# A two-block transformer step on one core: the weight ring begins 32 bytes lower, at a multiple of 64 bytes

## The chip, the cores and the metric

One core of a Trainium2 chip runs the program. The metric is the time of one execution on the device in microseconds (us). Three runs of the kernel before were timed; their median is 1489.44 us.

## The reference

256 tokens of width 1024 pass, in float32, through two blocks that follow one another. The first has a mixer (windowed attention with sinks and an HGRN recurrence, both gated, then `w_out`) and a layer of product-key experts: 128 x 128 experts, of which each token takes 8 x 16. The second has a mixer of three parts (gMLP, a convolution, an xLSTM cell), cross attention to a memory of 256 tokens, and a gated feed-forward of width 2816. Cut to the lines that make the large products:

```python
aq, ak, av, hq, hf, hi, hg, ga, gh = split_combined(h @ w_in)
merged = sigmoid(ga) * (y_attn @ w_attn_proj) + sigmoid(gh) * (y_hgrn @ w_hgrn_proj)
x = x + merged @ w_out
x = x + peer_layer(rms_norm(x, norm_ffn_g), w_peer_q, peer_keys, peer_u, peer_v)
...
h = h + hybrid_mixer(hn, w_in[l], ..., w_out[l])
h = h + cross_attention(hn, mn, w_xq[l], w_xkv[l], w_xo[l])
h = h + conv_glu(hn, w_up[l], conv_f_w[l], conv_f_b[l], w_down[l])
```

## The kernel before, in words

All weights, and all experts' rows (every expert is computed, the gates are zero where it isn't chosen), stream through the core as 448 tiles of 128 x 1024 float32 values, each of them a **slot** of work. A ring of pools holds them: four places `wraw` for what the sync queue loads, four places `wh` for the high part that ScalarE rounds off (float32r), three places `wl` for the rest that VectorE subtracts (`Slots`, L259). Every product is made of three matmuls in float32r, one for each of high x high, high x low and low x high; the second operand is kept in two tiles too, named with H and L. A slot of form `form2` or `formv` has 8 x 3 = 24 matmuls of 128 x 128 weights, taken from the ring, on 256 moving columns; `form2h` is the same with two halves of 512 rows. In `form1` it is the other way round: the activations are the weights of the array, and the ring tile is moved (the hi, av and mv slots, the last for the memory's values). Four of the memory's key slots (mk4 to mk7) use plain float32 and no split.

The activations that are moved: `hH`, `hL` (tile `hh`, L346), used by nearly all slots of the first block, by the experts and by most of the second; `yaH/L`, `yhH/L`, `mH/L` for pa, ph and wo of the first block; `yH/L`, `oH/L`, `h5H/L`, `fah/fal` for wo, xo, up (ug, uv) and down (dn) of the second; `hmH/L` for the memory. In the feed-forward the first up slots still move `hH/L`, and from the sixth on `h5H/L`.

The order in which the instructions are issued is worked out beforehand by a planner with estimated times of the engines (`Clock`, L117; pieces of work beside the slots are generators, `go` and `step`). It doesn't look at addresses. L219 is the helper through which nearly every instruction is recorded, so lines say little in the profile, and tiles are told apart by their names. Before the first slot 40 records of products of `ident` with itself run on TensorE (`WARM`, L353 to L356).

Where the tiles lie in a partition, in bytes, as the program allocates them (each tile is rounded up to 32 bytes; `con` comes first, the ring `wp` behind it, then the pools of the stages; a second stack of pools, with `hm` and the keys and values of the memory in it, is filled from the upper end and does not depend on what lies below):

| tile | first byte | modulo 64 | modulo 256 |
|---|---|---|---|
| x | 16512 | 0 | 128 |
| sm (265 columns, 1060 bytes) | 24704 | 0 | 128 |
| hH, hL | 25792, 33984 | 0 | 192 |
| ones_d (1 column) | 42176 | 0 | 192 |
| ident | 42208 | 32 | 224 |
| wraw, wh, wl (4096 bytes each) | 44000, 60384, 76768 | 32 | 224 |
| h5H, oH, second yH; h5L, oL, mL; fah, fal; yL | 89056; 97248; 118752, 121824; 121056 | 32 | 224 |
| yaH, yaL | 122432, 126528 | 0 | 64 |
| yhH, yhL; mH | 167616, 171712; 184000 | 0 | 192 |
| hmH, hmL (upper stack) | 192992, 201184 | 32 | 224 |

The 128 columns of a weight operand are 512 bytes of a partition, the 256 moving columns 1024 bytes, and the slices of a tile begin at multiples of these, so a slice lies as its tile does.

Of the kernel before, what the change touches and what calls it, by code (L numbers as in the profile page):

```python
# [22 lines left out]
F32 = mybir.dt.float32  # L23
# [6 lines left out]
PSUM = bass.MemoryType.PSUM  # L30

T = 256
# [27 lines left out]
# the weight tiles in the order of their use  # L60
# [22 lines left out]
# products of the memory are float32 ones, which take TensorE longer but spare the other engines the splits  # L83
# [24 lines left out]
# log1p(z) / z on [0, 1], relative error 3e-8  # L108
# [4 lines left out]
# y: bits of v -> a first guess of v ** -0.5; y * (w * (w + b) + a) with w = v * y * y comes within 2e-5 of it  # L113
# [3 lines left out]
class Clock:  # L117
    """Estimated times of the engines (ns), by which the order of issue is chosen."""

    # from the end of an instruction to the begin of one that depends on it: the own engine, PE, others  # L120
# [16 lines left out]
    def new(self, ap):  # L137
        """a tile takes the place of an older one of its tag"""
        t = ap.tensor
        if ap.name not in self.floor:  # L140
            ring = self.ring.setdefault(t.tag, [])
            f = 0.0
            if len(ring) >= (t.tag_meta.bufs or 1):
                old = ring.pop(0)
                f = max([r[4] for r in self.writes.pop(old, [])] + [r[4] for r in self.reads.pop(old, [])] + [0.0])
            ring.append(ap.name)
            self.floor[ap.name] = f
            self.writes[ap.name], self.reads[ap.name] = [], []
# [9 lines left out]
    def start(self, e, out, ins):  # L158
        """when an engine could begin"""
        t = self.t[e]  # L160
        for ap in ins + [out]:
            self.new(ap)
        for ap in ins:
            s = self.span(ap)
            for r in self.writes.get(ap.name, ()):
                if self.over(r, s) and not (e == "PE" and r[5] == "PE"):
                    t = max(t, r[4] + self.lat(r[5], e))
        s = self.span(out)
        t = max(t, self.floor[out.name])
        for recs in (self.writes, self.reads):  # L170
            for r in recs.get(out.name, ()):
                if r[5] != e and self.over(r, s):
                    t = max(t, r[4] + self.lat(r[5], e))
        return t
# [34 lines left out]
class Engine:  # L209
    """Hands instructions on to an engine and keeps its estimated clock."""  # L210
# [48 lines left out]
class Slots:  # L259
    """The stream of weight tiles: loads and splits run ahead of the products."""  # L260
# [43 lines left out]
    def done(self, n):  # L304
        """slot n has been issued"""
        if self.raw.pop(n, None) is not None:
            self.dma(len(self.seq))


def build(tc, xT, memT, smalls, smalls2, w1, keysT, uT, vT, w2, outT, stop=None):  # L310
# [22 lines left out]
    x = con.tile([128, 8, T], F32, name="x")  # L333
    sm = con.tile([128, NSM], F32, name="sm")
# [12 lines left out]
    ones_d = con.tile([128, 1], F32, name="ones_d")  # L347
# [5 lines left out]
    # products of nothing while the first loads are under way: they raise the clock of TensorE  # L353
# [8 lines left out]
    def go(g, late=1, eng="VS"):  # L362
        """start a piece of work that is issued bit by bit between the products; what it yields names the
        engines that the next bit is for"""
# [11 lines left out]
    def step(force=False):  # L376
        """issue what is ready by now, as far as the engines keep up"""
# [20 lines left out]
    def tt(out, a, b, op):  # L398
        """elementwise on SBUF: on the engine that is done first"""
# [7 lines left out]
    def until(*keys, eng=None):  # L407
        """for a generator: wait for what others issue"""
# [9 lines left out]
    class Sem:  # L418
        """PSUM tiles of one tag that generators may hold across slots"""
# [20 lines left out]
    def take_v(k=2):  # L440
        """banks for a product over several slots"""
# [20 lines left out]
    def slot(name, mm, evac):  # L462
        """one weight tile: mm(w) -> psum, evac(psum)"""
# [19 lines left out]
    def form2p(a):  # L483
        """float32 products, without splits"""
# [9 lines left out]
    def form2h(a):  # L494
        """two column tiles of a 512-row weight"""
# [9 lines left out]
    def form1(a, pv, i, e, width):  # L505
        """e contraction chunks of `width` columns; pv[t] accumulates over the tiles, both in one bank when they fit"""
# [19 lines left out]
    def pair(names, a, evacs, then=None, block=1, order=range(8), key=None):  # L526
        """two slots whose products alternate per chunk, for operands that are just being made"""
# [14 lines left out]
        # of the last chunks the low parts come last  # L542
# [32 lines left out]
    def formv(acc, a, first, last):  # L575
        """acc[n, t] += w[:, n]^T a, one chunk of the contraction"""
# [26 lines left out]
    def stat_mm(pc, sqs, first=True, last=True):  # L603
        """token sums: pc[t, i] += sum over partitions, for the two halves of the tokens"""
# [8 lines left out]
    def rsqrt_cols(dst, src, e, scale=1.0, E=None):  # L613
        """(src * scale + e) ** -0.5 on a few columns"""
# [4 lines left out]
    def rsqrt_of(dst, vv, E):  # L619
        """vv ** -0.5: a first guess from the bits, a step of third order and one of Newton's"""  # L620
# [25 lines left out]
    def rows_of(dst, cols, n=2):  # L646
        """dst[:, k * 128 + t] = cols[t, k] on all partitions"""
# [5 lines left out]
    # The products run on x * g; 1 / rms scales what comes out of them, until the operand has been  # L653
    # replaced by the normalized one (or for all products of a norm).
# [5 lines left out]
    class Norm:  # L660
        """The scale of a norm: products that come before it is known are scaled when it is."""
# [12 lines left out]
        def chain(self, sqs, e=EPS):  # L674
            """a generator: from the squares to the scale"""
# [24 lines left out]
        def when(self, f, late=1):  # L700
            """start f(rst) as soon as there is one"""
# [5 lines left out]
        def to(self, dst, *fs, late=1):  # L707
            """evacuation, and what to start then"""
# [21 lines left out]
        def renorm(self, src, g, np_):  # L730
            """a generator: the normalized operand, to be put in place of the other one"""
# [11 lines left out]
        def renorm_to(self, src, g, pool, dst, flag):  # L743
            """a generator: the normalized operand in a place of its own"""
# [10 lines left out]
        def write(self, must=False):  # L755
            """between two slots, when the operand is there"""
# [9 lines left out]
    class Sums:  # L766
        """sum over chunks of the squares, for chunks that come one by one"""
# [24 lines left out]
    def residual(n, sums, g, scale=None, key=None):  # L792
        """evacuation that adds to the stream; the operand and the squares of the next norm follow"""
# [23 lines left out]
    # ================= first block: mixer =================  # L817
# [14 lines left out]
    # attention bias: -slope * distance inside the window, -1e30 outside  # L832
# [9 lines left out]
    # scan reset: zero where a chunk of 32 begins  # L842
# [3 lines left out]
    # [s, t]: t >= s in the same chunk of 32  # L846
# [136 lines left out]
    def g_hgrn():  # L983
# [9 lines left out]
        # twice silu; the norm takes care of the factor  # L993
# [20 lines left out]
    def g_hpair(g):  # L1014
# [77 lines left out]
        # half of 1 / rms(po / 2), for the doubled gate  # L1092
# [76 lines left out]
    # the gates are (1 + tanh(z / 2)) / 2; the half follows where the products of wo come out  # L1169
# [51 lines left out]
    # ================= first block: product-key experts =================  # L1221
# [34 lines left out]
    def top16(vals, idx, src, n):  # L1256
        """the 16 largest of each row of the two sources, sorted, and their places"""
# [61 lines left out]
    # the two lists are sorted, so the best 16 sums lie where (a + 1)(b + 1) <= 16: rows 0..3 whole,  # L1319
    # and four columns of rows 4..15  # L1320
# [44 lines left out]
    def g_decode(t):  # L1365
        """key numbers of the chosen pairs"""
# [7 lines left out]
        # rows 0..3: a = pos >> 4, b = pos & 15; after them a = pos >> 2 less 12, b = pos & 3  # L1374
# [61 lines left out]
    def onehots(g):  # L1436
# [4 lines left out]
        for q in range(NG):  # L1441
            i2, gg = idxT[1][:, t + q:t + q + 1], idxT[2][:, t + q:t + q + 1]
            if q % 2 and clock.t["S"] < clock.t["V"] + 500:
                # g * max(1 - |j - i2|, 0)
# [82 lines left out]
    # for the sums of x ** 2 and (x * g4) ** 2  # L1527
# [23 lines left out]
    # keep t >= s  # L1551
# [10 lines left out]
    # the weights of the gates, split  # L1562
# [41 lines left out]
    # ================= second block: mixer =================  # L1604
# [12 lines left out]
    def finish(c0, c1):  # L1617
        """the sums of the experts: stream, operand and squares"""
# [16 lines left out]
    def g_norm3():  # L1635
        """the last norm of the first block and the first of the second"""
        # of x * r1 * g4 with r1 = (m1 + e) ** -0.5 the norm's scale is (r1 ** 2 * m2 + e) ** -0.5, together
        # (m2 + e * (m1 + e)) ** -0.5
# [45 lines left out]
    def gates():  # L1684
        """input and forget gates, tokens on partitions"""
# [12 lines left out]
    def g_gt(p):  # L1698
# [11 lines left out]
        # log sigmoid: min(x, 0) - log1p(exp(-|x|)); log1p(z) / z by a polynomial on [0, 1], to 3e-8  # L1710
# [40 lines left out]
    # causal depthwise convolution along time, taps w[:, 0..n-1]  # L1751
# [17 lines left out]
    def g_xc(h):  # L1769
# [11 lines left out]
        # twice silu  # L1781
# [20 lines left out]
    # conformer: convolution shared between VectorE and GpSimd, group standardize, silu  # L1802
    yb = [mp.tile([128, T], F32, name=f"bg{i}") for i in range(2)]

    def ev_tanh(dst, key, scale=0.5):
        """tanh(z / 2) + 1, which is twice the sigmoid"""
# [14 lines left out]
    # the gates are doubled, the taps halved  # L1821
# [65 lines left out]
    # gMLP  # L1887
# [42 lines left out]
    # xLSTM cell, one head  # L1930
# [155 lines left out]
    # ================= second block: cross attention =================  # L2086
# [72 lines left out]
    # ================= second block: gated feed-forward =================  # L2159
# [96 lines left out]
def _cols(v, n):  # L2256
    """[n*128] -> [128, n]"""
# [3 lines left out]
def _form2(w):  # L2261
    """[K, N] -> [N/128 tiles][128][K/128 * 128]"""
# [4 lines left out]
def _form1(w):  # L2267
    """[1024, N] -> [tiles][128][c, N] with 1024/N chunks per tile"""
# [5 lines left out]
def pack(inp):  # L2274
# [26 lines left out]
    # head i beside head i + 4  # L2301
# [18 lines left out]
    def taps(a, n):  # L2320
        """[K, n*128] -> [128, n*K]"""
# [66 lines left out]
```

## Time and profile before

| | |
|---|---|
| runs | 1487.21, 1489.44, 1493.71 us (median 1489.44) |
| span of the profiled execution | 1484.4 us; its time with what lies around the span is not given |
| TensorE: matmuls in flight, weight loads in flight | 1447.5 us, 1420.5 us |
| VectorE, ScalarE, GpSimd busy | 1076.2, 849.9, 181.4 us |
| transfers | 242.64 MB, 163 GB/s over the span |

The span is from the first to the last instruction. TensorE's matmuls and weight loads are pipelined: a record is longer than the distance to the next one, so rows of the timeline are read here by their first column, the time at which an instruction starts. Records name out<-moving,weights.

### The profile page before, as it was taken

How to read it: one execution, taken by the hardware profiler on the slowest of the kernel's cores; microseconds unless marked ns; L12 is line 12 of the kernel's file. 1: busy time of each engine (PE TensorE's matmuls, PEld its weight loads, DVE VectorE, ACT ScalarE, POOL GpSimd, SP SyncE). 2: the span in 40 equal slices, each digit the busy share in tenths (PEclk: the TensorE clock that was granted, in tenths of full speed). 3: DMA queues.
4: the chain of work that ended last, by engine and by line, in shares of the span. 5: the costliest groups of instructions: out<-in, count | busy, mean ns of one | idle time of the engine just before them, and what ended most of it. 6: DMA issues, size and time to landing. Idle time of an engine off the chain costs nothing. (4 is left out here: it accounts for less than half of the span.)

```text
span 1484.4 us, 30208 instructions
## 1 busy us (share of the span) xinstructions
PE 1447.5 (98%) x11904; PEld 1420.5 (96%) x11904; DVE 1076.2 (73%) x2096; ACT 849.9 (57%) x1617; POOL 181.4 (12%) x228
## 2 busy tenths in 40 slices
PE   8999999999999999999999999999999999999997
PEld 8789999999999999999999999999998899999996
DVE  7866579799888999955555566555699774785665
ACT  4754454454699988844444455444575544654553
POOL 6100032014200000000000030000035420410000
PEclk9999999999999999999999999999999999999998
DMA  6334554555544444455666665666542553556552
GB/s 217 128 114 157 171 185 153 175 172 182 161 141 143 143 143 143 142 180 172 185 188 185 227 198 185 186 185 186 168 129 81 162 159 114 170 185 187 183 184 73
DMA packets 66381, 242.64 MB, mean 163 GB/s; under 512 B 7360, under 2 KB 7488, under 8 KB 65856
## 3 DMA queue, kind: packets, MB, share of 16 engines
q1 hardware_dynamic: 65664, 237.01, 50.4%
q0 software_dynamic: 432, 3.58, 0.7%
q8 instruction: 93, 1.52, 0.4%
q14 instruction: 48, 0.39, 0.1%
q10 hardware_dynamic: 144, 0.14, 0.1%
HBM read 239.64 MB, written 1.05 MB: 162 GB/s over the span
## 5 line engine op out<-in xcount | busy, mean ns | idle before, releaser
L219 ACT CAST wh<-wraw 128x1024 fp32r<-128x1024 f32 x444 | 463.5, 1045 | 239.0 <-PE v L219 119.1
L219 DVE TENSOR_TENSOR wl<-wraw,wh 128x1024 fp32r<-128x1024 f32 x444 | 555.3, 1254 | 57.4 <-issue 41.0
L219 PE MATMUL v<-hH,wh 128*128 128x256 f32 x2048 | 587.0, 287 | 0.8 <-ACT hH L219 0.8
L219 PE MATMUL v<-hH,wl 128*128 128x256 f32 x2048 | 577.7, 282 | 1.4 <-DVE wl L219 1.3
L219 PE MATMUL v<-hL,wh 128*128 128x256 f32 x2048 | 576.6, 282 | 1.9 <-POOL hL L219 1.8
L219 PEld LDWEIGHTS v<-hL,wh 128*128 128x128 f32 x2048 | 386.2, 189 | 3.1 <-POOL hL L219 2.8
L219 PEld LDWEIGHTS v<-hH,wl 128*128 128x128 f32 x2048 | 386.3, 189 | 2.9 <-DVE wl L219 2.6
L219 PEld LDWEIGHTS v<-hH,wh 128*128 128x128 f32 x2048 | 386.9, 189 | 1.0 <-ACT hH L219 1.0
L219 PE MATMUL mm<-hH,wh 128*128 128x256 f32 x656 | 189.6, 290 | 6.7 <-DVE au L219 3.8
L219 PE MATMUL mm<-hH,wl 128*128 128x256 f32 x656 | 184.6, 282 | 2.2 <-DVE wl L219 2.2
L219 PE MATMUL mm<-hL,wh 128*128 128x256 f32 x656 | 183.0, 283 | 3.0 <-DVE hL L219 2.5
L219 PEld LDWEIGHTS mm<-hH,wh 128*128 128x128 f32 x656 | 124.5, 190 | 11.6 <-issue 4.6
L219 PEld LDWEIGHTS mm<-hL,wh 128*128 128x128 f32 x656 | 123.5, 190 | 4.2 <-DVE hL L219 3.1
L219 PEld LDWEIGHTS mm<-hH,wl 128*128 128x128 f32 x656 | 124.3, 189 | 2.8 <-DVE wl L219 2.8
L219 DVE TENSOR_TENSOR hL<-bigA,hH 128x256 fp32r<-128x256 f32 x72 | 31.2, 434 | 85.1 <-ACT hH L219 85.1
L219 PE MATMUL mm<-h5H,wh 128*128 128x256 f32 x272 | 77.0, 283 | 0.0
L219 PE MATMUL mm<-h5L,wh 128*128 128x256 f32 x272 | 77.0, 283 | 0.0
L219 PE MATMUL mm<-h5H,wl 128*128 128x256 f32 x272 | 77.0, 283 | 0.0
L219 DVE TENSOR_TENSOR hL<-bigB,hH 128x256 fp32r<-128x256 f32 x56 | 23.7, 425 | 69.0 <-ACT hH L219 69.0
L219 ACT ACTIVATE ohB<-ohB,gT,ngT 128x128 f32<-128x128 f32 x126 | 62.3, 494 | 4.2
L219 ACT ACTIVATE bigA<-v 128x256 f32<-128x256 f32 (+14 forms) x72 | 25.7, 357 | 68.1 <-PE v L219 68.1
L219 DVE TENSOR_TENSOR ohA<-iota,i1T 128x256 f32<-128x256 f32 x128 | 53.8, 420 | 14.0 <-PE aux L219 6.8
(545 smaller groups left out, 2414.2 us busy)
## 6 DMA issues: line engine op xcount, KB each, us to landing
wraw<-w_dram SPq DMA_DIRECT2D x192, 512.0 KB, 3.6
wraw<-uT_dram SPq DMA_DIRECT2D x128, 512.0 KB, 3.6
wraw<-vT_dram SPq DMA_DIRECT2D x128, 512.0 KB, 3.6
s2t<-smalls_dram POOLq DMA_DIRECT2D x1, 1444.0 KB, 10.9
x<-xT_dram SPq DMA_DIRECT2D x4, 256.0 KB, 6.0
kyT<-keysT_dram POOLq DMA_DIRECT2D x1, 1024.0 KB, 7.1
xm<-memT_dram POOLq DMA_DIRECT2D x1, 1024.0 KB, 5.8
outT_dram<-z SPq DMA_DIRECT2D x4, 256.0 KB, 2.6
```

Source lines behind the costliest of these rows:

```text
L219: r = f(out, *a, **k)
```

## The change

The column `ones_d`, which holds 1/1024 and is multiplied with squares to sum them over the partitions, had a tile of its own between `hL` and `ident`. It becomes column 265 of the tile `sm`, whose 266 columns (1064 bytes) are rounded up to the same 1088 bytes as before. So `ident` and all that lies behind it, the ring `wp` and the pools of the stages with it, begin 32 bytes lower: the ring at 43968, 60352 and 76736 (modulo 64: 0; modulo 256: 192), the tile behind it at 89024. `x`, `sm`, `hH`, `hL` and the upper stack stay. The load of `sm` writes the first 265 columns only. All comments and docstrings are removed too, with empty lines in their place. The diff without these:

```diff
-    sm = con.tile([128, NSM], F32, name="sm")
+    smo = con.tile([128, NSM + 1], F32, name="sm")
+    sm = smo[:, 0:NSM]
     nc.scalar.dma_start(sm, smalls)
...
     hh = (con.tile([128, 8, T], F32R, name="hH"), con.tile([128, 8, T], F32R, name="hL"))
-    ones_d = con.tile([128, 1], F32, name="ones_d")
+    ones_d = smo[:, NSM:NSM + 1]
     V.memset(ones_d, 1.0 / D)
```

## Rows read from the trace of the kernel before

**Rows 1.** The page, part 1: busy time, share of span, instructions.
```profile
PE 1447.5 (98%) x11904; PEld 1420.5 (96%) x11904; DVE 1076.2 (73%) x2096; ACT 849.9 (57%) x1617; POOL 181.4 (12%) x228
```
**Rows 2.** Windows: stretch, its length, busy us and instructions by engine, clock, DMA, GB/s.
```profile
222.00:395.00 173.00, 167.87 (x1387) 165.31 (x1386) 160.44 (x494) 82.17 (x132) 45.23 (x23) 0.99 0.54 170
395.00:690.00 295.00, 294.99 (x2515) 294.78 (x2513) 250.18 (x514) 239.68 (x570) 0.00 (x0) 1.00 0.48 150
```
**Rows 3.** Groups of TensorE: shapes, count, busy us, mean ns, idle before.
```profile
L219 PE MATMUL v<-hH,wh 128*128 128x256 f32 x2048 | 587.0, 287 | 0.8 <-ACT hH L219 0.8
...
L219 PE MATMUL mm<-hH,wh 128*128 128x256 f32 x656 | 189.6, 290 | 6.7 <-DVE au L219 3.8 <-DVE x L219 0.8 <-DVE q L219 0.7
...
L219 PE MATMUL mm<-h5H,wh 128*128 128x256 f32 x272 | 77.0, 283 | 0.0
```
**Rows 4.** Timeline of TensorE (start us, length us): feed-forward slots with hH, first and last.
```profile
1309.29 0.28 PE L219 MATMUL mm<-hH,wh 128*128 128x256 f32 x1
...
1314.85 0.28 PE L219 MATMUL mm<-hH,wl 128*128 128x256 f32 x1
```
**Rows 5.** Timeline of TensorE: the next two up slots, with h5H, first and last.
```profile
1317.83 0.28 PE L219 MATMUL mm<-h5H,wh 128*128 128x256 f32 x1
...
1323.47 0.28 PE L219 MATMUL mm<-h5H,wl 128*128 128x256 f32 x1
```
**Rows 6.** Timeline of TensorE: value slots of the memory, third, ninth and last.
```profile
1167.82 0.28 PE L219 MATMUL mm<-wl,hmH 128*128 128x256 f32 x1
...
1168.53 0.28 PE L219 MATMUL mm<-wl,hmH 128*128 128x256 f32 x1
...
1171.77 0.28 PE L219 MATMUL mm<-wl,hmH 128*128 128x256 f32 x1
```
**Rows 7.** Timeline of TensorE: av slots, third matmul and last.
```profile
1099.20 0.28 PE L219 MATMUL mm<-wl,hH 128*128 128x256 f32 x1
...
1101.65 0.28 PE L219 MATMUL mm<-wl,hH 128*128 128x256 f32 x1
```
**Rows 8.** Timeline of weight loads: 28 of st (32 moving columns), and the next.
```profile
99.19 3.21 PEld L219 LDWEIGHTS aux<-hq,st 128*128 128x128 f32 x28
102.32 0.19 PEld L219 LDWEIGHTS mm<-hH,wh 128*128 128x128 f32 x1
```
**Rows 9.** Timeline of weight loads: hH, hL under 16 or 8 columns, second and last.
```profile
1072.70 0.19 PEld L219 LDWEIGHTS aux<-gw,hL 128*128 128x128 f32 x1
...
1076.04 0.19 PEld L219 LDWEIGHTS aux<-gw,hL 128*128 128x128 f32 x1
```
**Rows 10.** The page, part 5: the subtraction that makes wl.
```profile
L219 DVE TENSOR_TENSOR wl<-wraw,wh 128x1024 fp32r<-128x1024 f32 x444 | 555.3, 1254 | 57.4 <-issue 41.0
```
**Rows 11.** Timeline of all engines at the start.
```profile
0.86 0.06 DVE L219 MEMSET ones_d<- 128x1 f32 x1 [0.86 <-PEq L2379]
...
1.45 7.00 PE L356 MATMUL aux<-ident 128*128 128x128 f32 x40 [1.45 <-DVE ident L219]
...
5.21 1.04 POOL L219 TENSOR_TENSOR sq<-x 128x512 f32<-128x512 f32 x1 [4.07 <-DMA x<-xT_dram]
...
9.40 2.52 POOL L219 TENSOR_TENSOR sq<-x 128x512 f32<-128x512 f32 x2 [0.97 <-DMA x<-xT_dram]
```
**Rows 12.** Transfers: out<-in, queue, count, KB each, median us from issue to landing.
```profile
wraw<-w_dram SPq DMA_DIRECT2D x192, 512.0 KB, 3.6
...
sm<-smalls_dram ACTq DMA_DIRECT2D x1, 132.5 KB, 4.5
```
**Rows 13.** Timeline of TensorE: pa slots, first matmul and last (96).
```profile
132.13 0.28 PE L219 MATMUL mm<-yaH,wh 128*128 128x256 f32 x1
...
143.52 0.28 PE L219 MATMUL mm<-yaH,wl 128*128 128x256 f32 x1
```
**Rows 14.** Timeline of TensorE: first ph slot, first matmul and last (24).
```profile
157.84 0.28 PE L219 MATMUL mm<-yhH,wh 128*128 128x256 f32 x1
...
160.56 0.28 PE L219 MATMUL mm<-yhH,wl 128*128 128x256 f32 x1
```

## The prediction

> **What bounds the kernel now.** I read the page's busy shares first: TensorE has a matmul in flight for 98% of the span and a weight load for 96%, VectorE is at 73% [rows 1]. A busy TensorE need not be a TensorE at its best, so the second view is the windows by stage. [...] So the end is set by how closely matmuls follow one another, and the third view is the timeline of TensorE alone, read for the distance between the starts of neighbours (the "spacing"). Nearly all matmuls are of one shape, 128x128 weights and 256 moving columns. Of these 3 x 2048 + 3 x 656 = 8112 move hH or hL against ring weights; 3 x 272 move h5H or h5L [rows 3]. By the code, at 24 matmuls a slot, the 22 down slots move fah and fal (528), and 8 slots each move yH/yL and oH/oL (384 together). A nanosecond of spacing on the 8112 is 8.1 us.
>
> **The change part by part.** No engine instruction is added or taken away. What changes is where operands lie. In what follows "even" means beginning at a multiple of 64 bytes, "odd" at 32 past one. Before, every ring tile is odd, hH and hL are even and don't move; h5, fa, y and o are odd and become even; the even operands of the first block (ya, yh, mH) become odd. The trace of before holds three of the four combinations of moving operand and weights in the same shape:
> - moving even, weights odd: 47 steps take 1314.85 - 1309.29 = 5.56 us, 118.3 ns each [rows 4];
> - moving odd, weights odd: in the very next pair of slots, same code with h5 in place of hH, 47 steps take 5.64 us, 120.0 ns each [rows 5]; the memory's value slots, where the ring moves and hmH/hmL are the weights, settle, after 6 steps of 118.3 (0.71 us), at 27 steps in 3.24 us, again 120.0 [rows 6];
> - moving odd, weights even: the av slots, same code as the value slots but with hH/hL as weights, 21 steps in 2.45 us, 116.7 [rows 7].
>
> So even weights were worth 120.0 - 116.7 = 3.3 ns, an even moving operand 120.0 - 118.3 = 1.7 ns. Even with even does not occur in this shape; it is what the change makes of the 8112. The lower bound is the spacing where next to nothing moves and only weight loads set the pace: 28 loads of st, odd, in 102.32 - 99.19 = 3.13 us, 111.8 ns [rows 8], and 30 steps of even hH/hL weights in 3.34 us, 111.3 [rows 9]. These two also say that alone a weight load does not care where it begins; the loss arises where both operands are read at once. The upper bound is 120.0 [rows 5]: it could even get worse. I take the sum of the two effects, 118.3 - 3.3 = 115.0 ns, as both neighbours of the missing corner (116.7 and 118.3) lie below the odd-odd corner and nothing in the rows shows the two gains to exclude one another. It follows:
> - the 8112: 8112 x 3.3 ns = 26.8 us less;
> - h5, fa, y, o go from odd-odd to even-even: (816 + 528 + 384) x 5.0 ns = 8.6 us less;
> - pa, ph and the first wo (16 slots, 384 matmuls) gain 3.3 by the weights and lose 1.7 by the moving operand: 0.6 us less;
> - the memory's slots and the hi and av slots (hm doesn't move, the ring does): 4 split key slots of 24 x 3.3 ns; 8 value and 2 av slots of 24 and 4 hi slots of 12 x 1.7 ns: 0.8 us less.
>
> Together 36.8 us, all on the path, since TensorE is the path. What is late next: VectorE. From 395 us on it has 15% and more to spare. From 222 to 395 us it has 7%; there 1387 matmuls x 3.3 ns = 4.6 us are to be won, and I give back half, 2.3 us, as sorting steps come one behind the other. Left: 34.5 us.
>
> The splits write and read the ring too: 444 subtractions of 1254 ns on VectorE [rows 10]. No row shows one with even tiles, so I take no change; if they moved by as much as the matmuls, 4%, either way, it would be 1387 / 24 = 58 slots x 1.254 us x 4% = 2.9 us in the tight stage, and nothing elsewhere. The loads land 3.6 us after issue [rows 12], with four tiles in the ring at 24 x 118.3 ns = 2.84 us a slot, so a slot of 24 x 115.0 = 2.76 us still finds its tile.
>
> The constant column: its memset runs at 0.86 us today, ahead of ident, and ident ahead of the 40 warming products of 7.00 us in TensorE's order [rows 11]. If the wait were set by whole tiles, the memset would have to wait for the load of sm, which lands 4.5 us after its issue [rows 12], so at 4.5 us at the earliest, and ident, the warming products and the first real product behind them would slip by 4.5 - 0.9 = 3.6 us or a little more. But the parts of x, loaded by four transfers into one tile, release their readers one by one, at 5.21 and at 9.40 us [rows 11]; parts of a tile are followed separately, and the column is no part of what is loaded. I take 0, with some 4 us as the upper end, at 1 in 10.
>
> Sum against the profiled execution: its span is 1484.4 us; what lies around it isn't given for that execution, but the median of the three runs, 1489.44, is 5.0 us above. 1484.4 - 34.5 = 1449.9, and 5.0 on top 1454.9: **1455 us**, 2.3% less. By the two bounds of the missing corner: at 111.6 ns 8112 x 6.7 + 1728 x 8.4 ns and some 5 us for the rest are 74 us, less about 7 that VectorE keeps, so 1422 us; at 120.0 ns 8112 x 1.7 = 13.8 us more, 1503 us.
>
> **The rivals.**
> *No change, 1489 us.* The differences of 1.7 and 3.3 ns could come from the order of the products or from which buffers are filled meanwhile. For it: the value slots run 6 steps at 118.3 before they settle at 120.0 [rows 6], so the spacing has a history and not only an address; and ya, which is even, runs at (143.52 - 132.13) / 95 = 119.9 ns [rows 13], not 118.3 as hH and as yh, in the same form of slot, with 23 steps in 2.72 us [rows 14]. Against it: 120.0 is exact over 48 matmuls in a row and hH has 118.3 in the neighbouring slots.
> [...]
> *Slower, 1503 us.* What counts is not where each operand begins but how far they are apart, modulo 256 bytes: the two readers then meet in the same part of the memory in step. By the addresses, h5, fa, y and o lie 0 from the ring, modulo 256, and so do hmH/hmL: all at 120.0. hH and yh lie 32 before it (118.3), the av slots 32 behind (116.7), and ya 96 behind, at 119.9, which the even-or-odd reading doesn't explain [rows 13]. The change moves the ring by 32 and leaves hH: they then lie 0 apart, and 8112 matmuls go to 120.0, while h5, fa, y, o keep their distance and their 120.0: 8112 x 1.7 ns = 13.8 us more. It decides as soon as the even-even corner is over 118.3. [...]
> *Only one effect pays, 1470 to 1481 us.* Even weights alone (116.7 for 118.3 on the 8112, 3.3 on the 1728): 13.0 + 5.7 us less, 1471; less still if VectorE takes back more.
> *No loss left, 1422 us*: the bound of rows 8 and 9.
>
> **How the numbers follow.** 1455 and about it (1443 to 1470) has a chance of 0.50; one effect alone 0.10; no loss left 0.05; no change 0.18; slower 0.17. So faster by over 0.5% 0.65, within 0.5% 0.18, slower by over 0.5% 0.17; 0.5%, some 7 us, is about what a measurement of this kernel can tell from no change. The range from 1425 to 1492 leaves out the slower case and a part of the lowest.
>
> **What would show it.** In the timeline, the hH slots of the feed-forward at 115.0 ns and the h5 slots at the same value; the expert stage without holes and shorter by 2.8%; VectorE's share in the sorting stage up; hH and h5 alike at 120.0 would show the slower rival, 118.3 and 120.0 unchanged the first one; warming products that start past 5 us would show the wait on sm. The forecast is wrong if the even-even spacing lies outside 113 to 117 ns, or if holes appear before wl in TensorE's timeline that eat what the spacing gives.

## The result, and the profile after

The changed kernel takes 1500.76 us (median of 6 runs, 1496.32 to 1504.55), the kernel before 1490.17 us (median of 6). The ratio is 1.0066, with a 95% interval of 1.0045 to 1.0087: some 10 us slower, where 1455 us had been forecast. The profiled execution's span is 1494.8 us, 10.4 us more than before, and every engine gets its instructions in the same order: only addresses differ.

Page, part 1, of the kernel after (engine, busy us, share of the span, instructions); it answers to [rows 1]:
```profile
PE 1459.5 (98%) x11904; PEld 1433.6 (96%) x11904; DVE 1076.2 (72%) x2096; ACT 849.1 (57%) x1617; POOL 181.5 (12%) x228
```
The extra time is TensorE's own, 1459.5 - 1447.5 = 12.0 us; VectorE and ScalarE do what they did. Two stretches of the kernel after in the windows view, beside [rows 2]:
```profile
222.00:395.00 173.00, 167.61 (x1369) 165.49 (x1369) 160.16 (x493) 81.03 (x129) 45.77 (x23) 0.99 0.53 165
395.00:690.00 295.00, 295.00 (x2504) 295.00 (x2503) 250.32 (x516) 240.26 (x574) 0.00 (x0) 1.00 0.49 150
```
In the same 173 us TensorE has 1369 matmuls in flight at some time where it was 1387; VectorE's share, which was to rise, doesn't (160.16 for 160.44). In the expert stage, still without a hole, 2504 for 2515. The granted clock is what it was (0.99 and 1.00).

TensorE's timeline after (start us, length us): the two up slots with hH, the two with h5, the value slots, the av slots, pa and ph, each by its first and its last matmul; they answer to [rows 4 to 7] and [rows 13, 14]:
```profile
1319.59 0.28 PE L219 MATMUL mm<-hH,wh 128*128 128x256 f32 x1
...
1325.23 0.28 PE L219 MATMUL mm<-hH,wl 128*128 128x256 f32 x1
...
1328.23 0.28 PE L219 MATMUL mm<-h5H,wh 128*128 128x256 f32 x1
...
1333.87 0.28 PE L219 MATMUL mm<-h5H,wl 128*128 128x256 f32 x1
...
1178.20 0.28 PE L219 MATMUL mm<-wl,hmH 128*128 128x256 f32 x1
...
1182.10 0.29 PE L219 MATMUL mm<-wl,hmH 128*128 128x256 f32 x1
...
1109.66 0.28 PE L219 MATMUL mm<-wl,hH 128*128 128x256 f32 x1
...
1112.18 0.28 PE L219 MATMUL mm<-wl,hH 128*128 128x256 f32 x1
...
134.07 0.28 PE L219 MATMUL mm<-yaH,wh 128*128 128x256 f32 x1
...
145.47 0.29 PE L219 MATMUL mm<-yaH,wl 128*128 128x256 f32 x1
...
159.99 0.28 PE L219 MATMUL mm<-yhH,wh 128*128 128x256 f32 x1
...
162.71 0.28 PE L219 MATMUL mm<-yhH,wl 128*128 128x256 f32 x1
```
These rows decide most of the case. The reader divides each difference by its steps and sets beside it the distance of the two operands, moving minus weights, modulo 256 bytes:

| slots | steps | distance before, after | spacing before, after (ns) |
|---|---|---|---|
| hH (rows 4) | 47 | 224, 0 | 118.3, 120.0 |
| h5 (rows 5) | 47 | 0, 0 | 120.0, 120.0 |
| value slots (rows 6) | 33 | 0, 224 | 120 (settled), 118.2 |
| av (rows 7) | 21 | 32, 0 | 116.7, 120.0 |
| pa, with ya (rows 13) | 95 | 96, 96 | 119.9, 120.0 |
| ph, with yh (rows 14) | 23 | 224, 224 | 118.3, 118.3 |

Where both operands moved together (h5, ya, yh) nothing changed, though "odd" and "even" changed places. Where one moved, the spacing is that of the new distance: hH has taken over h5's 120.0, the value slots hH's old 118.2.

By stage, cut at the same work in both kernels (the first product of the sorting, the first and last ohB product, the first gw product), the windows of the kernel before:
```profile
214.37:393.24 178.87, 173.00 (x1429) 170.27 (x1427) 166.95 (x517) 83.74 (x132) 45.69 (x23) 0.99 0.53 168
393.24:627.74 234.50, 234.50 (x2006) 234.50 (x2005) 215.66 (x469) 211.66 (x527) 0.00 (x0) 1.00 0.46 143
627.74:1072.69 444.95, 443.09 (x3739) 442.16 (x3738) 256.05 (x358) 218.25 (x343) 14.42 (x31) 1.00 0.60 187
```
and of the kernel after:
```profile
216.71:396.77 180.06, 174.67 (x1429) 172.41 (x1427) 166.94 (x517) 83.28 (x132) 45.77 (x23) 0.99 0.54 167
396.77:632.10 235.33, 235.33 (x2005) 235.33 (x2004) 215.80 (x469) 211.66 (x527) 0.00 (x0) 1.00 0.47 142
632.10:1082.96 450.86, 448.79 (x3740) 448.00 (x3738) 255.62 (x358) 218.10 (x343) 14.52 (x31) 1.00 0.60 185
```
The sorting takes 1.2 us more, the first half of the expert stage 0.8, its second half 5.9; of the remaining 2.5 us, 1.9 lie ahead of pa, where this execution's granted clock was 0.97 on average and that of before 1.00. Over the whole kernel I averaged the steps of up to 130 ns that follow a matmul of hH or hL: 118.49 ns before (7820 steps), 119.78 after (7797). 8112 x 1.29 = 10.5 us, as much as the spans differ. The steps can also be paired, since the order is the same: the 11260 that last up to 130 ns in both traces are 10.2 us longer together, 10.0 of it behind hH and hL, and all others sum to 0.2 us. So the spacing is the whole of the difference between the two profiled executions.

### The profile page after: what moved, and what is told of

Its sections match the earlier page's. It is cut to its first block, busy times and chain, and to the rows that moved or that the text cites. A ratio compares the mean times of both kernels' runs of the same rounds, so it can differ in the third digit from the quotient of the medians.

```text
span 1494.8 us, 30208 instructions
## 1 busy us (share of the span) xinstructions
PE 1459.5 (98%) x11904; PEld 1433.6 (96%) x11904; DVE 1076.2 (72%) x2096; ACT 849.1 (57%) x1617; POOL 181.5 (12%) x228
## 5 line engine op out<-in xcount | busy, mean ns | idle before, releaser
L219 PEld LDWEIGHTS v<-hL,wh 128*128 128x128 f32 x2048 | 392.7, 192 | 3.2 <-POOL hL L219 2.9
L219 PEld LDWEIGHTS v<-hH,wl 128*128 128x128 f32 x2048 | 392.1, 191 | 2.0 <-DVE wl L219 1.9
L219 PEld LDWEIGHTS v<-hH,wh 128*128 128x128 f32 x2048 | 392.3, 192 | 1.0 <-ACT hH L219 1.0
L219 PEld LDWEIGHTS mm<-hH,wh 128*128 128x128 f32 x656 | 127.8, 195 | 11.0 <-issue 4.5
L219 PEld LDWEIGHTS mm<-hL,wh 128*128 128x128 f32 x656 | 126.9, 195 | 4.2 <-DVE hL L219 3.0
L219 PEld LDWEIGHTS mm<-hH,wl 128*128 128x128 f32 x656 | 127.7, 195 | 1.5 <-DVE wl L219 1.5
```

The costliest lines, as they stand in the source:

```text
L219: r = f(out, *a, **k)
```

## The experiments

Two theories were set against each other. *Distance*: the spacing depends on how far the two operands lie apart, modulo 256 bytes. *Own start* (the prediction's reading): it depends on whether each begins at an even or odd multiple of 32. Others are named where they were tried.

**The spacing by itself, first table.**
```
for name, form, wo, mo in MAP:          # 39 pairs of starts, all twice
    for k in range(96):
        c, q = k // 3 % 8, k % 3
        PE.matmul(p, w[:, a:a + 128], h[:, b:b + 256], ...)
    PE.matmul(g, ident, ident, ...)     # between two groups
```


> This kernel leaves the whole computation out and measures the disputed cost by itself: groups of 96 matmuls (128x128 weights, 256 moving columns, the order of chunks and of high and low parts as in a slot), no other engine at work, each group with its own start of the weights and of the moving operand, in bytes past a multiple of 256; two passes over the list. Distance (modulo 256, moving minus weights): all groups of one distance have one spacing, whatever their absolute start: 120.0 ns at 0, 118.3 at -32 (224), 116.7 at +32, about 119.9 at -96 (160), the other distances open, and the even or odd start counts for nothing. Absolute start (the prediction's reading): weights at 0 with the moving operand at multiples of 64 all 115.0; weights at 32 with it at odd multiples of 32 all 120.0. Traffic of other engines (what is read as address is in truth the loads and the splits): all groups alike, near 112 to 116 ns. With only one chunk in use (groups called one), distances of 256, 512 and 768 behave as 0 if the modulus is 256, otherwise they differ.

Timeline of TensorE in this kernel; a row is a group of 96. Its length holds the last matmul's own 0.28 us and a first step of 0.20 us, so the spacing is (length - 0.48) / 94. In order: both at 0; weights 0 and moving 32; both at 32; weights 32 and moving 224; then one chunk only, 0, 256 and 288 apart:
```profile
17.61 11.76 PE L82 MATMUL w_m__141<-H,W 128*128 128x256 f32 x96
...
29.34 11.45 PE L82 MATMUL w_m__240<-H,W 128*128 128x256 f32 x96
...
110.36 11.76 PE L82 MATMUL w_m__933<-H,W 128*128 128x256 f32 x96
...
180.02 11.15 PE L82 MATMUL w_m__1527<-H,W 128*128 128x256 f32 x96
...
377.06 11.76 PE L82 MATMUL one_w_m__3210<-H,W 128*128 128x256 f32 x96
...
388.80 11.76 PE L82 MATMUL one_w_m__3309<-H,W 128*128 128x256 f32 x96
...
435.43 11.55 PE L82 MATMUL one_w_m__3705<-H,W 128*128 128x256 f32 x96
```
Even with even (first row) and odd with odd (third) have 120.0 alike; even weights give anything from 116.7 to 120.0. The mean of the last 48 steps by distance 0, 32, ... 224: 120.0, 116.7, 117.8, 120.0, 118.6, 118.6, 117.8, 118.3, the same with the weights at 0 and at 32 within 0.1 ns, but for one: distance 192 with the weights at 32 has 113.3 (fourth row, 113.5 with its beginning). One chunk at distances of 256, 512 and 768 has 120.0 as at 0, and at 544 and 800 it has 116.7 as at 32, so the modulus is 256. One group doesn't fit as it stands: 288 (last row) has 117.8 in both passes and not 116.7; 117.8 comes back below as a second value of 32. The kernel gives no other engine any work in these groups, so the spread from 113.3 ns at 192 to 123.3 at 4 arises among TensorE's own matmuls and weight loads. The forecast of 119.9 for distance 160 was my slip of sign: ya lies at 96, where the table has 120.0, as rows 13 have.

**The column alone.**
```
+    pad = con.tile([128, 8], F32, name="pad")
     ones_d = smo[:, NSM:NSM + 1]
```


> The changed kernel with 32 bytes left free ahead of ident: the constant column lies in the tile of the loaded parameters as in the change, but the ring and the pools behind it stay where they were before. Distance or absolute start: as before, 1490 us, ratio 0.998 to 1.002. If the column itself costs (its memset waits for the load of the parameters, 4 us in my estimate): 1494, and a slip of the warming products in the trace.

1490.55 us, ratio 0.9992 (0.9975 to 1.001): the column costs nothing that can be measured. In the trace of the change its memset still runs at 0.86 us and the warming products begin at 1.45:
```profile
0.86 0.06 DVE L219 MEMSET sm<- 128x1 f32 x1 [0.86 <-PEq L2380]
...
1.45 6.93 PE L357 MATMUL aux<-ident 128*128 128x128 f32 x40 [1.45 <-DVE ident L219]
```

**hH moved, the ring left alone.**
```
-    smo = con.tile([128, NSM + 1], F32, name="sm")
+    smo = con.tile([128, NSM + 9], F32, name="sm")
```


> The changed kernel with 32 bytes more in the tile ahead of hH: hH and hL begin 32 bytes higher, the ring and everything behind it lie where they were before the change. So the ring hasn't moved, and hH and the ring lie 0 apart, both at odd multiples of 32. Distance: as slow as the change, ratio 1.005 to 1.008, hH slots of the feed-forward at 119.4 to 120.0 ns, yh at 118.3. If the slowdown comes from the ring's or the lower pools' own place (loads, splits, copies): as before, ratio 0.998 to 1.002, hH slots at 118.3. The even-or-odd reading of the prediction: odd with odd, 120.0, so slower too.

1500.42 us, ratio 1.0052 (1.0034 to 1.007). TensorE's timeline, the up slots with hH:
```profile
1324.14 0.28 PE L219 MATMUL mm<-hH,wh 128*128 128x256 f32 x1
...
1329.78 0.28 PE L219 MATMUL mm<-hH,wl 128*128 128x256 f32 x1
```
5.64 us in 47 steps, 120.0 again. So the slowdown of the change comes back without moving the ring, the loads or the lower pools: what makes it is the distance of hH from the ring. (Own start, odd with odd, would have said the same; the next two part them.)

**All starts by all starts, second table.** As the first, with 8 x 8 starts, 72 matmuls a group, in two passes.

> This kernel too leaves the whole computation out: the table of all 8 starts of the weights by all 8 starts of the moving operand (multiples of 32 past 256), 72 matmuls in the order of a slot for each, twice: pass x with 2 passes of a float32 product of 128 columns between the groups, pass y with 6 of 96 columns, so that the groups begin out of another beat. If distance alone decides: one value to each diagonal of the table, as in the first map: 120.0 at 0, 116.7 at +32, 117.8 at +64 and +192, 120.0 at +96, 118.6 at +128 and +160, 118.3 at +224, in both passes. If the beat out of which a group begins counts as well (the one 113.3 of the first map, against 117.8 at the same distance): some cells of a diagonal differ, and differ between the passes, most of all at +192; the 120.0 of distance 0 holds in all 16 cells. The prediction's even-or-odd reading: no such pattern can come out, since even-even and odd-odd lie on the same diagonals.

Timeline of TensorE; a name gives pass, start of the weights, start of the moving operand (A to H for 0 to 224). Here the spacing is (length - 0.48) / 70:
```profile
17.36 8.88 PE L71 MATMUL x_wAmA<-H,W 128*128 128x256 f32 x72
26.22 8.65 PE L71 MATMUL x_wAmB<-H,W 128*128 128x256 f32 x72
...
43.55 8.87 PE L71 MATMUL x_wAmD<-H,W 128*128 128x256 f32 x72
...
69.93 8.72 PE L71 MATMUL x_wAmG<-H,W 128*128 128x256 f32 x72
...
96.11 8.88 PE L71 MATMUL x_wBmB<-H,W 128*128 128x256 f32 x72
104.96 8.65 PE L71 MATMUL x_wBmC<-H,W 128*128 128x256 f32 x72
...
631.45 8.43 PE L71 MATMUL y_wAmG<-H,W 128*128 128x256 f32 x72
```
Settled (mean of the last 24 steps), distance 0 has 120.0 in 16 of 16 groups, 32 has 116.7, 64 has 117.8, 96 has 120.0 and 224 has 118.3, each in all 16. Two distances have two values: 160 has 118.6 to 118.8 or 117.2 to 117.4 (8 groups each), 192 has 117.8 or 113.3 (7 and 9). The very pair A, G has the one in pass x and the other in pass y, so the addresses alone don't pick between them. The passes differ in what runs between the groups; that this sets a beat which picks the value is a reading, and no run tried it by itself. Own start falls here: even with even and odd with odd share the distances 0, 64, 128 and 192, and those run from 113.3 to 120.0.

**Parity as before, distance 32.**
```
+    for _ in range(2):
+        con.tile([128, 2], F32, name="sd", bufs=2)
     hh = (con.tile([128, 8, T], F32R, name="hH"), ...
+    pad = con.tile([128, 8], F32, name="pad")
```


> The ring and all behind it lie as before the change; two 8-byte columns (sd) move from behind hL to ahead of hH, and the constant column lies with the parameters: hH and hL begin 64 bytes higher, even as before, the ring odd as before, but hH now lies 32 ahead of the ring, modulo 256, and not 32 behind. Distance: hH slots at 116.7 instead of 118.3 ns, 8112 x 1.67 = 13.5 us less, some 1477 us, ratio 0.990 to 0.993; with part of it kept by VectorE in the sorting stage 0.995. Even or odd: nothing changes, ratio 0.998 to 1.002, hH slots at 118.3.

1484.08 us, ratio 0.9956 (0.9937 to 0.9975): own start said no change. The feed-forward's slots settle at 117.9, not 116.7 (5.54 us in 47 steps), and the mean over all hH steps is 117.24: the distance of 32 too has a second value, 117.8, which the third table shows in one pass and the first at 288. So faster by distance, but half as much as forecast.

**Parity as after, distance 64.** The same without the pad.

> The changed kernel with the same two columns moved ahead of hH: the ring even and hH even, as in the change, but 64 apart instead of 0. Distance: 117.8 ns, 8112 x 0.55 = 4.5 us less than before, ratio 0.996 to 0.999, against 1.0066 of the change. Even or odd (an even-even pair is as slow as the change showed it): 1.005 to 1.008.

1486.82 us, ratio 0.9946 (0.992 to 0.9973). Even with even, as in the change, and faster than before, as distance 64 says. The ratio is a little below the forecast 0.996 to 0.999, which its interval reaches; the mean step is 117.54, where 117.8 had been taken. TensorE's timeline, up slots with hH:
```profile
1315.83 0.28 PE L219 MATMUL mm<-hH,wh 128*128 128x256 f32 x1
...
1321.37 0.28 PE L219 MATMUL mm<-hH,wl 128*128 128x256 f32 x1
```
5.54 / 47 = 117.9. With this own start is out: the same parity gave 120.0 in the change.

**Distance 192 for hH.**
```
+    for n in ("rsv", "rst_", "rsu"):
+        for _ in range(2):
+            con.tile([128, 4], F32, name=n, bufs=2)
     hh = (con.tile([128, 8, T], F32R, name="hH"), ...
```


> The changed kernel with six 16-byte columns (rsv, rst_, rsu) moved from behind hL to ahead of hH: hH and hL begin 192 bytes higher, even, the ring even as in the change, 192 apart. Distance, by the second table, where this distance has two settled values: 113.3 ns if the slots fall into the short one (8112 x 5.0 = 40 us less than before, less what VectorE keeps: ratio 0.973 to 0.980), 117.8 if into the long one (4.5 us less, 0.997); a mixture lies between. Even or odd: 1.005 to 1.008, as the change.

1470.31 us, ratio 0.9846 (0.9815 to 0.9876), a mixture of the two values: mean 115.15 ns over the hH steps, h5 still at 120.0.

**Distance 192 for both.**
```
+    con2 = es.enter_context(tc.tile_pool(name="con2", bufs=1))   # opened behind wp
...
-    t = con.tile([128, 4], F32, name="rst_", bufs=2)[:, 0:n]
+    t = con2.tile([128, 4], F32, name="rst_", bufs=2)[:, 0:n]    # rsv, rsu too
```


> The changed kernel with the same six columns in a pool of their own between the ring and the pools behind it: hH stays, the ring begins 192 bytes lower, the lower pools lie as in the change. So hH lies 192 from the ring, modulo 256, and h5, fa, y, o lie 192 from it too, not 0. Distance: as h192 for the 8112, and another 1728 x 2.2 ns = 3.8 us (117.8) to 1728 x 6.7 = 11.5 us (113.3) less: ratio 0.965 to 0.995, h5 slots of the feed-forward at 117.8 or 113.3 instead of 120.0. Even or odd: 1.005 to 1.008, h5 at 120.0.

1457.02 us, ratio 0.9753 (0.9714 to 0.9792). hH's mean is 114.07; h5 has left 120.0 for the long value, 117.8.

**Distance 32 for both.** sd goes into spare columns of the parameters' tile, with one pad of 32 bytes ahead of the ring and one behind it.

> sd lies with the parameters, 32 bytes are left free ahead of ident and 32 behind the ring: the ring is odd, hH even, h5, fa, y, o even, and both lie 32 ahead of the ring, modulo 256. Distance: hH as in h32 (measured there 0.9956), and h5, fa, y, o at 116.7 instead of 120.0 ns, 1728 x 3.3 = 5.8 us less: ratio 0.990 to 0.993, h5 slots at 116.7. Even or odd: h5 gains 1.7 ns only, 2.9 us, hH nothing: 0.998.

1475.4 us, ratio 0.9888 (0.9863 to 0.9914). Timeline of TensorE, two slots with h5:
```profile
1318.82 0.28 PE L219 MATMUL mm<-h5H,wh 128*128 128x256 f32 x1
...
1324.31 0.28 PE L219 MATMUL mm<-h5H,wl 128*128 128x256 f32 x1
```
5.49 / 47 = 116.8 where all kernels with distance 0 have 120.0. The ratio lies just under the forecast 0.990 to 0.993: hH too is at 116.78 here, where the kernel from which the forecast took it has 117.24.

**Distances in steps of 8 bytes, third table.**

> The third table, with the whole computation left out again: distances in steps of 8 bytes from 0 to 248, 72 matmuls each, in three passes that differ in the start of the weights (0, 96 and 192 past 256) and in what runs between the groups. If the distance counts in parts of 32 bytes, the four groups from one multiple of 32 on are alike; if it counts continuously, they differ, with 120.0 at 0 in every pass, and there may be a distance below 116.7 that doesn't have two settled values, as 192 does (113.3 and 117.8). From the first map: 123.3 at 4, 118.7 at 16, 118.3 at 48, 120.0 at 80, 119.2 at 208, 117.1 at 240.

Timeline of TensorE, pass x at distances 72, 112 and 192, pass y at 136, and 112 and 192 in pass z:
```profile
96.22 9.01 PE L71 MATMUL x_Cb<-H,W 128*128 128x256 f32 x72
...
140.66 8.46 PE L71 MATMUL x_Dc<-H,W 128*128 128x256 f32 x72
...
228.72 8.43 PE L71 MATMUL x_Ga<-H,W 128*128 128x256 f32 x72
...
456.03 8.89 PE L71 MATMUL y_Eb<-H,W 128*128 128x256 f32 x72
...
730.21 8.45 PE L71 MATMUL z_Dc<-H,W 128*128 128x256 f32 x72
...
826.96 8.72 PE L71 MATMUL z_Ga<-H,W 128*128 128x256 f32 x72
```
The distance counts in steps finer than 32: settled values run from 113.3 (112; its rows of 8.46 us give 114.0 with the beginning) to 122.2 (136, in passes x and z; 120.0 in pass y). Only 112 has 113.3 in all three passes; 192 has it in two (pass z: 8.72, so 117.7), and 16 and 144 have it in pass z alone, where x and y have 118.7 to 118.8. So two values are no peculiarity of 160 and 192: the passes also part at 8, 32, 56 and 128. The value of 0 is 120.0 in all three.

**Distance 112 for both.**
```
-    hh = (con.tile([128, 8, T], F32R, name="hH"), con.tile([128, 8, T], F32R, name="hL"))
+    hb = con.tile([128, 16 * T + 8], F32R, name="hH")
+    hh = [hb[:, 4 + 8 * T * i:4 + 8 * T * (i + 1)].rearrange("p (c t) -> p c t", t=T) for i in range(2)]
...
+    def late(p, n, name, **kw):          # h5, fah, fal, oH, oL
+        return p.tile([128, n + 64], F32R, name=name, **kw)[:, 60:60 + n]
```


> hH and hL become one tile with 16 bytes ahead (so hL appears under the name hH in the trace); rst_ and rsu lie behind the ring; h5, fa and o get 240 bytes ahead of them in their tiles. By the addresses hH, hL, h5, fa, fal and o then lie 112 from the ring, modulo 256, the distance that had 113.3 ns in all three passes of the third table, and y lies 128 from it. Distance: the 8112 at 113.3 for 118.5 (42 us less), 816 + 528 + 192 at 113.3 for 120.0 (10 us less), less what VectorE keeps in the sorting stage: 1440 to 1452 us, ratio 0.966 to 0.975, hH and h5 slots of the feed-forward both at 113.3. If the table only holds where no other engine touches the memory: a mixture of 113 to 118, ratio 0.975 to 0.99. If starts at 16 past a multiple of 32 cost the writers of hH: holes ahead of the hH slots that eat the gain.

1453.65 us, ratio 0.9745 (0.9727 to 0.9762), the fastest. TensorE's timeline, up slots with hH and with h5:
```profile
1285.86 0.39 PE L219 MATMUL mm<-hH,wh 128*128 128x256 f32 x2
...
1291.18 0.28 PE L219 MATMUL mm<-hH,wl 128*128 128x256 f32 x1
...
1302.50 0.28 PE L219 MATMUL mm<-h5H,wh 128*128 128x256 f32 x1
...
1307.82 0.28 PE L219 MATMUL mm<-h5H,wl 128*128 128x256 f32 x1
```
5.32 / 47 = 113.2 for both: the table holds inside the kernel. Yet 1453.65 is just above the forecast of 1440 to 1452. Step by step against before, the 11198 steps that last up to 130 ns in both traces are 45.2 us shorter, 35.4 of it behind hH and hL; expected were 42 + 10, but hH's mean is 113.94 and not 113.3. All other steps are 14.3 us longer together. The windows, cut at the same work, sorting, both halves of the expert stage, and the second block's mixer and attention:
```profile
216.33:393.29 176.96, 167.72 (x1428) 164.01 (x1427) 167.55 (x517) 84.05 (x132) 45.85 (x23) 1.00 0.55 170
393.29:621.12 227.83, 227.83 (x2005) 227.83 (x2004) 214.32 (x469) 211.14 (x526) 0.00 (x0) 1.00 0.49 147
621.12:1049.30 428.18, 425.38 (x3740) 424.41 (x3738) 255.75 (x358) 218.81 (x344) 14.71 (x31) 1.00 0.64 195
1049.30:1274.59 225.29, 215.08 (x1641) 205.29 (x1639) 166.68 (x337) 127.27 (x279) 71.07 (x120) 0.98 0.45 135
```
The expert stage is 6.7 + 16.8 us shorter than before, the sorting only 1.9: there VectorE is at 167.55 of 176.96 us, 95%, and TensorE waits in its place, 9.2 us without a matmul (176.96 - 167.72) where it was 5.9. Mixer and attention are no shorter (225.29 us; the same stretch of before, next fence), though their paired steps gain 3.3 us: the other steps lose 3.8, and 3.1 of that lies where the granted clock of one of the two executions was at its lower level (0.98 on average here, 0.99 before).
```profile
1072.69:1297.56 224.87, 215.25 (x1641) 205.50 (x1639) 166.81 (x337) 127.15 (x279) 71.38 (x120) 0.99 0.43 135
```
Of the 14.3 us, 3.4 are in the sorting, 3.8 in mixer and attention, 1.4 in the expert stage, 1.2 in the feed-forward behind its hH slots, and 4.4 ahead of pa. By the clock, 7.7 of them fall on steps that touch a stretch at the lower level in one of the two executions (the windows view of before gives a granted clock of 0.50 from 228.15 to 231.50 us): 4.6 ahead of pa, 3.1 in mixer and attention, about 1 in the feed-forward, and about 1 the other way in the sorting, where the trace of before has such a stretch and this one has none. So at an equal clock the sorting would keep 4.4 us. The stretch ahead of pa (135.0 us at a mean granted clock of 0.96, before 132.1 at 1.00) bears the clock out: with the starts of the ring and of hH as before (the kernel with the column alone) it took 133.2 at 0.99, and where hH lies 0 from the ring 134.1 at 0.97 (the change) and 138.4 at 0.94 (hH moved).

All kernels beside one another; the fourth column is what 8112 matmuls of hH and hL make by the mean step, the last what the ratio makes of 1490 us:

| kernel | distance of hH, h5 | mean hH step (ns) | hH's part (us) | ratio | us |
|---|---|---|---|---|---|
| before | 224, 0 | 118.49 | | 1 | |
| the change | 0, 0 | 119.78 | +10.5 | 1.0066 | +9.8 |
| hH moved | 0, 0 | 119.79 | +10.5 | 1.0052 | +7.7 |
| | 32, 0 | 117.24 | -10.1 | 0.9956 | -6.6 |
| | 64, 0 | 117.54 | -7.7 | 0.9946 | -8.0 |
| | 192, 0 | 115.15 | -27.1 | 0.9846 | -22.9 |
| | 32, 32 | 116.78 | -13.9 | 0.9888 | -16.7 |
| | 192, 192 | 114.07 | -35.9 | 0.9753 | -36.8 |
| | 112, 112 | 113.94 | -36.9 | 0.9745 | -38.0 |

In the last three h5, fa, y and o add their own (5 to 10 us), so of what the spacing gives, 2 to 3 us (distance 32), 4 to 5 (192) and 9 (112) don't arrive; only the 9 are more than the interval of their ratio (2.6 us either way). The trace shows 4.4 us of these in the sorting; where the rest stays is open. The clock doesn't account for it: the mean granted clock of the timed runs is 0.989 to 0.992 at distance 112 and about the same, 0.988 to 0.993, for the kernel before beside it.

## Why the prediction was wrong

- *What bounds the kernel*: right, as [rows 2] have it: in the expert stage TensorE had no hole (294.99 of 295 us) beside a VectorE at 85%, in the sorting VectorE was at 93%, and the granted clock was 1.00 and 0.99. TensorE's spacing is the path; the time moved its way in all eight kernels with another distance, if not always by all of it (distance 32 for hH: 6.6 us of 10.1).
- *The term for the 8112*: here it failed, in its sign. "I take the sum of the two effects, 118.3 - 3.3 = 115.0 ns" made two effects out of three corners and added them. The corners were three distances (224, 0, 32), and the fourth was no corner but distance 0 once more: 120.0. The measured mean is +1.29 ns, 10.5 us more, not 26.8 less.
- *h5, fa, y, o*, forecast at 115.0 from 120.0: unchanged, 120.0, as both operands moved together. *pa and ph*: unchanged, 120.0 and 118.3. The value slots gained and the av slots lost as distance says; a few tenths of a us.
- *The slower rival* (1503 us, chance 0.17) was the right one: hH and h5 alike at 120.0, with distance as the variable. That the two readers meet in the same part of the memory was its guess at the cause; no run shows it. Its price was 13.8 us, measured 10.5: in the first half of the expert stage the matmuls come in runs of 12 between ohB products, and before the change they had not settled at 118.3 but lay at 119.2 on average; they lost 0.2 ns there (to 119.4), and 1.6 in the second half (118.3 to 120.0).
- *The weighing*: the two effects together had a chance of 0.50, distance 0.17, though [rows 13] part the two readings: ya is even, has odd weights as hH does, and ran at 119.9, not 118.3. The own-start reading had no answer to it, and the text said so; a row that one theory explains and the other doesn't should have moved the chances.
- *The first rival* (no change, chance 0.18) was wrong: 1.0066, and the interval leaves out 1. Nor is every start at a multiple of 16 bytes as good as another: in pass x of the third table, with the weights at 0, moving operands at such multiples have 120.0 ns at distance 96, 113.3 at 112 and 118.7 at 128.
- *The column*: right, 0 (ratio 0.9992). *VectorE in the sorting*: it gave back nothing, as nothing was won; at distance 112 it kept more than the half that I had allowed: the paired steps there gave 5.3 us, and 3.4 of it didn't arrive, 4.4 at an equal clock.

## What to carry to other kernels

Where matmuls follow one another without holes, print for each form the start of the moving operand minus that of the weights, modulo 256, and the spacing, before moving a tile: here the spacing went with this distance, from 113.3 ns at 112 to 123.3 at 4, and not with alignment (with both operands at multiples of 64, the hH steps had a mean of 119.78 ns at distance 0 and 117.54 at 64). When a table of cases has an empty corner, look for one variable that orders all the filled ones, and for the row that only it explains, before adding two effects. A gain of 4% in TensorE's spacing (118.49 to 113.94 ns) was there for a few moved columns and some padding; the sorting, with VectorE at 95%, passed on only 1.9 of its 5.3 us.

## What the runs showed of the hardware

- With 128x128 weights and 256 moving columns, the spacing went with (moving - weights) modulo 256 bytes in the three tables: 120.0 ns at 0, 24, 88 and 96, 113.3 at 112, 123.3 at 4 (first table), 122.2 or 120.0 at 136, with no work for any other engine in the groups. Weight loads with 32 moving columns behind each followed one another at 111.8 [rows 8]; the warming products of the kernel before, in plain float32 with 128 moving columns, at 111.6 over their last 16 steps.
- Some distances have two settled values (192: 117.8 or 113.3; 160: 118.6 or 117.3; 16 and 144: 118.7 or 113.3; 32: 116.7 or 117.8), and in the second table the same pair of starts shows one in one pass and the other in the other. What picks between them, and where the period of 256 bytes comes from, stays open; no run here settles either.
- In the tables a matmul of 256 columns together with its weight load takes 1.5 to 11.5 ns (113.3 to 123.3) more than the 111.8 of loads beside 32 columns [rows 8], and how much goes with the distance of the two operands. What 256 columns take with no load beside them, no run here shows.
